# w_o by paired quarters, norm steps at fixed points, w_down by thirds of columns, and activations in eight DRAM buffers

## The chip, the cores and the metric

The kernel runs on one core of a Trainium2 chip. The metric is the device time of one execution in microseconds (us); less is better. The time before is the median of three executions. One further execution was recorded by the hardware profiler, and the trace and all rows shown are from that one.

## What is computed

One step of a one-layer decoder block on 1024 prompt rows and 8 x 4 sample rows, 1056 rows of 1024 values in all, in float32. The part that the change touches begins at `w_o`:

```python
def _rmsnorm(x, g):
    xf = x.astype(jnp.float32)
    y = xf * lax.rsqrt(jnp.mean(xf * xf, axis=-1, keepdims=True) + EPS)
    return (y * g.astype(jnp.float32)).astype(x.dtype)
...
    x = x + (g_a * y_a + g_b * y_b + g_m * y_m) @ w_o
    h = _rmsnorm(x, norm_ffn_g) @ w_up
    hc, conv_f_state = _causal_dwconv3(h, conv_f_prev, conv_f_w)
    hc = hc + conv_f_b
    a, gt = jnp.split(hc, 2, axis=-1)
    x = x + (jax.nn.silu(gt) * a) @ w_down
...
y_prompt = _rmsnorm(xp, norm_final_g)
```

`w_o` is 1024 x 1024, `w_up` 1024 x 5632, `w_down` 2816 x 1024. Ahead of this stand the input projections, a short convolution, a gated spatial mix and attention over 256 memory rows; the change leaves them as they are.

## The kernel before

**Matrix products.** Activations lie transposed: `S`, `zhi` and `zlo` hold 128 partitions x 8 feature tiles x 1056 rows. A float32 product is done as three float32r products. A weight tile is loaded to `ws`, ScalarE casts it to `wh` (L188), VectorE subtracts to get the rest `wl` (L190), and `three` (L210) issues `wh*xhi`, `wh*xlo` and `wl*xhi` (L211 to L213). So each weight unit costs one DMA on SyncE's queue, one ScalarE cast and one VectorE subtraction. `unit_cols` lists the units in order of use, `load_unit` loads them into a ring of three, `split_unit` casts them, `split_lows` subtracts, and `ahead` runs two units before use.

**What sets the order.** The program is written out by hand, and each engine and each DMA queue works through its own list in that order. Small items are put into a queue `aux` and taken out by `weave` between groups of matmuls, at a rate that `pace` sets; in the FFN, items are taken at fixed products.

**w_o.** Eight output tiles f of 128 columns. f 0 to 3 come first, each over three chunks of 352 rows (`main(wo_evac(f))`). `wo_evac` adds x (brought back from DRAM by `x_back`, L1067, on ScalarE's DMA queue), squares the sum on ScalarE and adds it to `acc` on GpSimd. f 4 to 7, whose split weights were kept in `wo`, follow by quarters of 264 rows in the order 0, 2, 1, 3, two tiles to one PSUM pair (`wo_pair`).

**The norm (`norm2`).** When a quarter is done, its items enter `aux`: `total` (L1216: TensorE sums the squares over partitions), `spread` (L1228: TensorE lays 1/rms over all partitions), `scale` (L1246, VectorE), and `parts` (L1254 cast on ScalarE, L1255 subtraction on VectorE). The FFN's product with `w_up` uses a scheme of seven products of half-size blocks in place of eight, so the quarters 2 and 3 also make differences of blocks (`minus`, L1259, GpSimd). `spread`'s PSUM tile and the outputs of `parts` are read by products 1 to 7 later on.

**The FFN.** There are 24 entries of seven products in the order `ORDER`; entries 0 to 3 are half entries (columns 0 and 1, for the first row half, then the second), the other 20 cover both. For each entry `raw_load` brings four blocks of `w_up`, `sums` makes three combinations on GpSimd (L1337 to L1339), `prepare` casts and subtracts four products ahead (L1350, L1351) and makes one more difference on GpSimd (L1354). `evacuate` moves products out of PSUM (L1444, L1446), `conv_items` is the convolution (L1386 to L1407), `gate_items` is the gate (L1419, L1420, L1424) and the store of an activation row to DRAM (`act_d`, L1425).

**w_down.** Four quarters of 264 rows; for each, four pairs of output tiles (q) by six groups of up to four activation rows (g), so 4 x 24 = 96 weight units. `stage_items` loads a group from `act_d` (L1530), and x from `x_d` with the fifth group (L1534); `part` casts and subtracts it (L1543, L1544). For the first quarter the groups are staged in two rows of `S` while the FFN's last entry runs (`at_last`).

**The end (`finish`).** Per quarter three pieces of 88 rows: eight transposes (L1615), a square with sum (L1619), `scales` (L1633, then `rsqrt`, L235 to L241), and the output multiply (L1644) and store. The last quarter's pieces run after the last product.

## Time and profile before

| | us |
|---|---|
| median of three executions | 1943.39 (1943.14 to 1945.38) |
| the profiled execution | 1948.35 |
| its span, first to last instruction | 1946.6 |
| TensorE busy in it | 1853.6 (95%) |
| VectorE | 1199.1 (62%) |
| ScalarE | 662.7 (34%) |
| GpSimd | 391.4 (20%) |

The span is cut into 40 equal slices below; each digit is the busy share of a slice in tenths (9 is 90% or more), and PEclk is the TensorE clock that was granted.

```profile
PE   8999999999999999999999667999999996999997
DVE  5576775328533753366361668898888886556654
PEclk9999999999999999999999887999999998999998
```

A slice is 48.7 us. TensorE (PE) is busy throughout except in the 23rd to 25th slice (1071 to 1217 us), where w_o ends, the norms run and the FFN begins, in the 34th (1606 to 1655), between the FFN and w_down, and at the two ends. The 23rd and the 24th slice, and the 25th, also have a lower clock.

### The profile page before, as it was taken

The numbers are of one execution on the slowest core, as the hardware profiler recorded it, in microseconds if no ns is written. First come the engines' busy times: TensorE is split into PE (matmuls) and PEld (weight loads), VectorE is DVE, ScalarE is ACT, GpSimd is POOL, SyncE is SP. The second block draws the span as 40 slices with busy tenths as digits, with TensorE's granted clock in tenths as the row PEclk, the third lists the DMA queues.
The fourth block names the chain that finished last, engine by engine and source line by source line (L and its number), as shares of the span: only waits on it lengthen the run. The fifth ranks groups of instructions, "written<-read, shape, count | busy, mean of one in ns | idle before, by whom it ended". The sixth has DMA issues, their size and how long they took to land.

```text
span 1946.6 us, 32112 instructions
## 1 busy us (share of the span) xinstructions
PE 1853.6 (95%) x13032; PEld 1824.7 (94%) x13032; DVE 1199.1 (62%) x2200; ACT 662.7 (34%) x1078; POOL 391.4 (20%) x475
## 2 busy tenths in 40 slices
PE   8999999999999999999999667999999996999997
PEld 8988999999999999999999667999999996899997
DVE  5576775328533753366361668898888886556654
ACT  6644313221322132112341223333433433344443
POOL 2221200000000000000002435665656651000000
PEclk9999999999999999999999887999999998999998
DMA  8736152133212521252141112322322315776764
GB/s 260 202 111 228 52 178 76 44 108 121 76 47 66 173 74 40 61 166 77 57 134 61 45 60 77 88 74 72 90 73 73 90 56 169 255 238 201 244 193 124
DMA packets 263443, 225.59 MB, mean 116 GB/s; under 512 B 8272, under 2 KB 248472, under 8 KB 263296
## 3 DMA queue, kind: packets, MB, share of 16 engines
q1 hardware_dynamic: 253383, 209.97, 35.4%
q10 hardware_dynamic: 9913, 13.57, 2.1%
q8 instruction: 102, 1.67, 0.4%
q14 instruction: 45, 0.37, 0.1%
HBM read 193.71 MB, written 29.81 MB: 115 GB/s over the span
## 4 chain that ended last, share of the span: by engine, by line
PE 60%; DVE 11%; POOL 10%; issue 9%; DMA 5%; ACT 4%; SPq 1%; ACTq 0%; DVEq 0%; POOLq 0%
PE mm L213 14%; PE mm L211 14%; PE mm L212 14%; PE pair L213 3%; PE pair L211 3%; PE pair L212 3%; DMA ws<-in_w_down 3%; POOL rs L1420 2%; POOL S L1339 2%; DVE wh L1351 2%; DVE wl L190 2%; POOL S L1338 1%; POOL S L1337 1%; POOL ext L1390 1%; POOL ws L1354 1%
## 5 line engine op out<-in xcount | busy, mean ns | idle before, releaser
L211 PE MATMUL mm<-zhi,wh 128*128 128x352 f32 x1824 | 591.9, 324 | 0.3 <-ACT zhi L273 0.3
L212 PE MATMUL mm<-zlo,wh 128*128 128x352 f32 x1824 | 589.5, 323 | 1.1 <-POOL zlo L284 1.0
L213 PE MATMUL mm<-zhi,wl 128*128 128x352 f32 x1824 | 588.4, 323 | 0.2 <-DVE wl L190 0.2
L190 DVE TENSOR_TENSOR wl<-ws,wh 128x1024 fp32r<-128x1024 f32 (+1 forms) x203 | 245.0, 1209 | 217.3 <-ACT wh L188 216.3
L211 PE MATMUL pair<-zhi,wh 128*128 128x264 f32 x1152 | 332.9, 289 | 24.0 <-ACT wh L188 17.0
L212 PEld LDWEIGHTS mm<-zlo,wh 128*128 128x128 f32 x1824 | 342.5, 188 | 2.7 <-POOL zlo L284 1.9
L211 PEld LDWEIGHTS mm<-zhi,wh 128*128 128x128 f32 x1824 | 343.1, 188 | 1.2 <-ACT zhi L273 0.6
L213 PEld LDWEIGHTS mm<-zhi,wl 128*128 128x128 f32 x1824 | 342.7, 188 | 0.5 <-DVE wl L190 0.5
L212 PE MATMUL pair<-zlo,wh 128*128 128x264 f32 x1152 | 331.2, 287 | 0.4 <-DVE zlo L1544 0.4
L188 ACT CAST wh<-ws 128x1024 fp32r<-128x1024 f32 x204 | 206.2, 1014 | 275.1 <-PE mm L212 101.8
L211 PEld LDWEIGHTS pair<-zhi,wh 128*128 128x128 f32 x1152 | 220.7, 192 | 25.4 <-ACT wh L188 17.4
L212 PEld LDWEIGHTS pair<-zlo,wh 128*128 128x128 f32 x1152 | 220.6, 192 | 0.6 <-DVE zlo L1544 0.6
L213 PE MATMUL pair<-zhi,wh 128*128 128x264 f32 x704 | 202.6, 288 | 0.0
L211 PE MATMUL pair<-fs,wh 128*128 128x264 f32 x536 | 158.1, 295 | 10.8 <-DVE rs L1444 6.1
L213 PEld LDWEIGHTS pair<-zhi,wh 128*128 128x128 f32 x704 | 135.3, 192 | 0.0
L213 PE MATMUL pair<-zhi,wl 128*128 128x264 f32 x448 | 128.9, 288 | 3.0 <-DVE wl L190 2.9
L211 PEld LDWEIGHTS pair<-fs,wh 128*128 128x128 f32 x536 | 102.8, 192 | 14.5 <-ACT wh L188 4.1
L844 DVE CUSTOM_DVE_ANT_0 qr<-fs,fs 128x256 f32<-128x256 f32 x256 | 108.4, 423 | 7.3
L212 PE MATMUL pair<-fs,wh 128*128 128x264 f32 x384 | 110.0, 286 | 0.0
L212 PE MATMUL pair<-rs,wh 128*128 128x264 f32 x356 | 102.4, 288 | 0.0
L213 PE MATMUL pair<-fs,wh 128*128 128x264 f32 x352 | 100.3, 285 | 0.0
L1130 ACT ACTIVATE sig<-mm 128x352 f32<-128x352 f32 x72 | 33.4, 464 | 186.9 <-PE mm L213 186.6
(334 smaller groups left out, 3200.6 us busy)
## 6 DMA issues: line engine op xcount, KB each, us to landing
ws<-in_w_in SPq DMA_DIRECT2D x88, 512.0 KB
ws<-in_w_down SPq DMA_DIRECT2D x80, 512.0 KB
fs<-q_d SPq DMA_DIRECT2D x32, 512.0 KB
ws<-in_w_up SPq DMA_DIRECT2D x54, 256.0 KB
act_d<-rs SPq DMA_DIRECT2D x21, 528.0 KB
S<-in_w_up SPq DMA_DIRECT2D x42, 256.0 KB
fs<-in_cache_mem_k SPq DMA_DIRECT2D x16, 512.0 KB
fs<-in_cache_mem_v SPq DMA_DIRECT2D x16, 512.0 KB
```

What stands on the lines that cost most here:

```text
L188: nc.scalar.copy(out=hi, in_=t)
L190: lows.append(lambda: eng.tensor_tensor(out=lo, in0=t, in1=f32(hi), op=ALU.subtract))
L211: mmul(ps, lhsT=wh, rhs=xh, start=first, stop=False)
L212: mmul(ps, lhsT=wh, rhs=xl, start=False, stop=False)
L213: mmul(ps, lhsT=wl, rhs=xh, start=False, stop=last)
L844: nc.vector.tensor_tensor_reduce(out=att["qr"], in0=q[:, i, :], in1=t[:, 2 * (bb % 2) + mt, :], scale=1.0, scalar=0.0, op0=ALU.mult, op1=A ...
L1130: nc.scalar.activation(out=t, in_=ps, func=AF.Sigmoid)
L1337: tt(out=s1, in0=a21, in1=a22, op=ALU.add)
L1338: tt(out=s2, in0=s1, in1=a11, op=ALU.subtract)
L1339: tt(out=a21, in0=a11, in1=a21, op=ALU.subtract)
L1351: nc.vector.tensor_tensor(out=lo, in0=a, in1=f32(hi), op=ALU.subtract)
L1420: nc.gpsimd.tensor_tensor(out=g[:, :T], in0=g[:, :T], in1=outs[j, 0][:, :T], op=ALU.mult)
```

## The change

Five parts, all behind the input projections.

1. **w_o by paired quarters.** Instead of four tiles over three chunks, then four tiles over four quarters, there are 32 steps of one tile and one quarter (24 matmuls of 264 columns). First quarters 0 and 2: tiles 0 to 3 in pairs of quarters, then tiles 4 to 7 for quarter 0 and for quarter 2. Then the same for quarters 1 and 3, for which tiles 0 to 3 are loaded and split a second time.
2. **Norm steps at fixed points.** `total`, `spread` and the other items stand at numbered steps (a table `todo` for w_o's steps, `ffn_first` for the FFN's products) and no longer in `aux`. For quarters 1 and 3, two of the four block differences run on VectorE.
3. **The FFN's order and places.** Products 2 and 6 change places; raw weights, sums and sigmoids of entries 4 and later lie in whole rows of `S`; entry 3 is handled like the entries before it.
4. **w_down by thirds.** Three thirds of 352 rows instead of four quarters: 72 weight units, not 96, and matmuls of 352 columns. `act_d` is eight tiles of up to three activation rows each, x is laid out in another way and is read back later, and the staged groups are eight of three rows.
5. **The end.** Pieces of 128, 128 and 96 rows, 9 in all instead of 12. The last three pieces share one `scales`, and two halves of their outputs are made by ScalarE and GpSimd and stored from ScalarE's queue.

The core of the diff:

```diff
-    for f in range(4):
-        unit_cols(w_o, f * P)
+    for f in range(8):
+        unit_cols(w_o, f % 4 * P)
...
-            head = [total, no, spread, scale(0, 0), scale(0, 1)]
             if not second:
-                return head + [parts(1, b11), scale(1, 0), scale(1, 1), parts(2, b21)]
-            return head + [
-                minus(b11, b12, b11),
+                return total, spread, [
+                    scale(0, 0), scale(0, 1), scale(1, 0), scale(1, 1), parts(1, b11), parts(2, b21)
+                ]
+            dve = nc.vector if s else nc.gpsimd
+            return total, spread, [
+                scale(0, 0), scale(0, 1),
+                minus(b11, b12, b11, dve),
                 scale(1, 0), scale(1, 1),
                 parts(3, b22),
-                minus(b12, b22, b12),
+                minus(b12, b22, b12, nc.gpsimd),
+                minus(b22, b22, b11, dve),
+                parts(6, b22),
                 parts(5, b11),
-                minus(b22, b22, b11),
+                minus(b21, b21, b22, nc.gpsimd),
                 parts(7, b12),
-                minus(b21, b21, b22),
-                parts(6, b22),
                 parts(4, b21),
             ]
 
...
+        def wo_pairs(f, s, ps):
+
+            until(lambda: len(back) == 3)
+            x = halves(S[:, f, :], s)
+            a = halves(acc[:, :T], s)
+            nc.vector.tensor_tensor(out=x, in0=ps[:, :, :QC], in1=x, op=ALU.add)
+            if f == 0:
+                nc.scalar.activation(out=a, in_=x, func=AF.Square)
+            else:
+                sq = squares()
+                nc.scalar.activation(out=sq, in_=x, func=AF.Square)
+                nc.gpsimd.tensor_tensor(out=a, in0=a, in1=sq, op=ALU.add)
+
...
-        ORDER = (1, 6, 2, 5, 7, 3, 4)
+        ORDER = (1, 2, 6, 5, 7, 3, 4)
...
-                    t = t[:, :, 0:P], t[:, :, P : 2 * P]
+                if half and e >= 4:
+                    t = v3(S[:, 6 + e % 2, :], KT, P)
...
-        act_d = dram.tile([NJ, P, T], F32, name="act_d")
-        x_d = dram.tile([4, P, KT, QC], F32, name="x_d")
+        act_d = [dram.tile([3, P, T], F32, name=f"act_d{i}") for i in range(8)]
+        x_d = dram.tile([P, KT, T], F32, name="x_d")
...
-        for f in range(4):
-            main(wo_evac(f))
-        drain()
...
+        norms = {c: norm2(c) for c in range(4)}
+
+        def plan_norm(at, c, first=0):
+
+            total, spread, items = norms[c]
+            slots = {(at, 2): [total], (at + 1, 2): [spread]}
+            for i, x in enumerate(items):
+                slots[at + 2 + i // 3, i % 3] = [x]
+            return slots
+
+        todo = {}
+        for at, c in ((12, 0), (16, 2), (28, 1)):
+            for key, gos in plan_norm(at, c).items():
+                todo.setdefault(key, []).extend(gos)
+        todo.setdefault((24, 0), []).append(lambda: sums(0))
+        todo.setdefault((22, 2), []).append(lambda: raw_load(0))
+        for i in range(6):
+            todo.setdefault((25 + i // 2, i % 2), []).append(lambda i=i: prepare(i + 1))
+
+        def wo_step(at, w, ps, c):
+            wh, wl = w
             r = quarter(c)
-            for f in (4, 6):
-                if f == 4:
-                    nc.sync.dma_start(out=x_d[c, :, 0:4, :], in_=S[:, 0:4, r])
-                ps = pair()
-                for x in range(2):
-                    wh, wl = wo[f + x]
-                    for k in range(KT):
-                        three(ps[:, x, :QC], wh[:, k, :], wl[:, k, :], zhi[:, k, r], zlo[:, k, r], k == 0, k == KT - 1)
-                        if k % 3 == 2:
-                            weave()
-                wo_pair(f, r, ps)
+            for k in range(KT):
+                three(ps, wh[:, k, :], wl[:, k, :], zhi[:, k, r], zlo[:, k, r], k == 0, k == KT - 1)
+                if k in (2, 5):
+                    split_lows()
+                    for go in todo.get((at, k // 3), ()):
+                        go()
+                    if at < 8:
+                        weave()
+
...
+        pace(24)
+        at = 0
+        for s in range(2):
+            order = [(f, c) for f in range(4) for c in (s, s + 2)]
+            if s == 0:
+                order = [(0, 0), (1, 0), (0, 2), (1, 2)] + order[4:]
+            ws, pss = {}, {}
+            if s:
+                drain()
+            for f, c in order:
+                if f not in ws:
+                    ws[f], pss[f] = next_unit(), pair()
+                    ahead()
+                wo_step(at, ws[f], pss[f][:, c // 2, :QC], c)
+                if c == s + 2:
+                    wo_pairs(f, s, pss[f])
+                wo_rest(at)
+                at += 1
+            for c in (s, s + 2):
+                nc.sync.dma_start(out=x_d[:, 0:4, quarter(c)], in_=S[:, 0:4, quarter(c)])
+            for c in (s, s + 2):
+                for f in range(4, 8):
+                    if f % 2 == 0:
+                        ps = pair()
+                    wo_step(at, wo[f], ps[:, f % 2, :QC], c)
+                    if f % 2:
+                        wo_pair(f - 1, c, ps)
+                        nc.sync.dma_start(out=x_d[:, f - 1 : f + 1, quarter(c)], in_=S[:, f - 1 : f + 1, quarter(c)])
+                    wo_rest(at)
...
-                    z = as4(st[g]) if c else block(S, g % 2, 3)
+                    st[g] = S[:, 6 + g % 2, :] if c == 0 else fs.get()
                     nc.sync.dma_start(
-                        out=z[:, :nk, :], in_=act_d[k0 : k0 + nk, :, quarter(c)].rearrange("k p t -> p k t")
+                        out=view(st[g], g),
+                        in_=act_d[g][: min(3, NJ - 3 * g), :, c * CH : (c + 1) * CH].rearrange("j p t -> p j t"),
                     )
-                    if g == 4:
-                        nc.sync.dma_start(out=S[:, :, quarter(c)], in_=x_d[c])
...
             go = {
-                1: [loads[0]], 6: [load_unit], 2: [splits[0], loads[2], load_unit],
-                7: [splits[2], loads[4], loads[1], load_unit], 3: [splits[1], loads[3]],
-                4: [splits[3], split_unit, split_lows],
+                1: [load_unit, load_unit, loads[0]],
+                5: [lambda: extra_free(6), splits[0], loads[1]],
+                7: [lambda: rows_free(0), load_unit, loads[2]],
+                3: [splits[1], loads[3], splits[2], loads[4], split_unit],
+                4: [lambda: extra_free(7), splits[3], split_lows, loads[5]],
             }
...
+        ffn_first = {}
+        total, spread, items = norms[3]
+        ffn_first[1] = [total]
+        ffn_first[3] = [spread]
+        for i, x in enumerate(items):
+            ffn_first.setdefault(4 + i, []).append(x)
+        POPS = {1: 1, 2: 2, 6: 1, 5: 1, 7: 1, 3: 1, 4: 1}
...
+            def x_again(c=c):
+                nc.sync.dma_start(out=S[:, :, c * CH : (c + 1) * CH], in_=x_d[:, :, c * CH : (c + 1) * CH])
+
             if c == 0:
-                at_slot(0, 0, left[0], splits[4])
-                for x, go in enumerate(left[1:]):
-                    at_slot(x // 5, x % 5, go)
-                at_slot(1, 2, loads[5])
-                at_slot(1, 4, splits[5])
+                for x, go in enumerate(left):
+                    at_slot(0, max(0, x - 3), go)
+                at_slot(0, 0, splits[4], loads[6])
+                at_slot(0, 1, splits[5])
+                at_slot(0, 2, splits[6])
+                at_slot(0, 4, loads[7])
+                at_slot(1, 1, splits[7])
+                at_slot(1, 2, x_again)
...
+                la = (12, 13, 14, 15, 16, 17, 19, 20) if c == 0 else (3, 5, 7, 9, 11, 13, 19, 20)
+                sa = (13, 14, 15, 16, 17, 18, 21, 22) if c == 0 else (5, 7, 9, 11, 13, 15, 21, 22)
+                for go, x in zip(nloads + nsplits, la + sa):
+                    at_slot(*divmod(x, 6), go)
...
-            scales(i)()
-            out(i, (slice(0, 512), slice(512, D)))()
+        scales(0, 3)()
+        for i in range(3):
+            out(i, ((0, 512, True), (512, D, i == 2)))()
```

Three places where the order of the instructions changes, each as the rows of one engine's or queue's list (source line, operation, out<-in, shape, xcount).

**ScalarE where w_o begins.** L1067 are the six DMAs that bring x back, L188 the casts of w_o's tiles 0 to 3, L1282 and L1299 the squares of tile 0. Before:

```order
L1067 DMA S<-xT_d 128x4x352 x2
L1130 ACTIVATE sig<-mm 128x352
L1150 CAST zhi<-S 128x4x352 x2
L188 CAST wh<-ws 128x1024
L1067 DMA S<-xT_d 128x4x352 x2
L1282 ACTIVATE fs_9653<-S 128x352 x2
L1067 DMA S<-xT_d 128x4x352 x2
L349 COPY fs_9721<-aux 72x128
L351 DMA out_new_conv_a_prompt<-fs_9721 2x4x128
```

And now:

```order
L1067 DMA S<-xT_d 128x4x352 x2
L1130 ACTIVATE sig<-mm 128x352
L1150 CAST zhi<-S 128x4x352 x2
L188 CAST wh<-ws 128x1024 x2
L1067 DMA S<-xT_d 128x4x352 x4
L1299 ACTIVATE fs_9653<-S 128x2x264
L1302 ACTIVATE fs_9654<-S 128x528
L188 CAST wh<-ws 128x1024
```

Two casts, of the third and the fourth tile, stand next to each other ahead of four of the six DMAs, where one cast stood ahead of two and the squares of two chunks ahead of the last two.

**GpSimd through w_o's end and the norms.** The additions of squares are L1286 and L1296 before, L1303 and L1313 now; the block differences L1259 and now L1251; `sums` L1337 to L1339 and now L1354 to L1356; the further difference L1354 and now L1371. Before:

```order
L1286 TENSOR_TENSOR fs_9653<-fs_9653,fs_9654 128x352 x9
L1296 TENSOR_TENSOR fs_9653<-fs_9653,fs_9654 128x264 x4
L1337 TENSOR_TENSOR fs_10266<-ws 128x4x128
L1338 TENSOR_TENSOR fs_10266<-fs_10266,ws 128x4x128
L1339 TENSOR_TENSOR ws<-ws 128x512
L1259 TENSOR_TENSOR S<-S 128x4x264
L1296 TENSOR_TENSOR fs_9653<-fs_9653,fs_9654 128x264 x2
L1259 TENSOR_TENSOR S<-S 128x4x264 x3
L1296 TENSOR_TENSOR fs_9653<-fs_9653,fs_9654 128x264 x2
```

And now:

```order
L1303 TENSOR_TENSOR fs_9653<-fs_9653,fs_9654 128x2x264 x3
L1313 TENSOR_TENSOR fs_9653<-fs_9653,fs_9654 128x264 x4
L1251 TENSOR_TENSOR S<-S 128x4x264
L1303 TENSOR_TENSOR fs_9653<-fs_9653,fs_9654 128x2x264
L1251 TENSOR_TENSOR S<-S 128x4x264 x3
L1303 TENSOR_TENSOR fs_9653<-fs_9653,fs_9654 128x2x264 x2
L1354 TENSOR_TENSOR fs_10447<-ws 128x4x128
L1355 TENSOR_TENSOR fs_10447<-fs_10447,ws 128x4x128
L1356 TENSOR_TENSOR ws<-ws 128x512
L1371 TENSOR_TENSOR ws<-ws,fs_10447 128x512
L1313 TENSOR_TENSOR fs_9653<-fs_9653,fs_9654 128x264 x4
```

The block differences of quarter 2 stand between the additions for tiles 0 to 3 of quarters 1 and 3, and the first entry's `sums` with the difference stand ahead of the additions (L1313) of quarters 1 and 3 for the tiles 4 and 5.

**The passage to w_down: ScalarE.** L1543 and now L1605 are the casts of staged activation groups, L188 those of w_down units, L1386 and now L1403 the convolution, L1419 and now L1436 the sigmoid. Before:

```order
L1543 CAST zhi<-S 128x4x264
L1350 CAST wh<-S 128x512
L1543 CAST fs_10319<-S 128x1056
L1419 ACTIVATE S<-rs_15901 128x4x264
L349 COPY fs_16013<-aux 72x128
L351 DMA out_new_conv_ffn_prompt<-fs_16013 2x4x128
L351 DMA out_new_conv_ffn_sample<-fs_16013 16x4x128
L1543 CAST zhi<-S 128x4x264
L1543 CAST fs_10632<-S 128x1056
L188 CAST wh<-ws 128x1024
L1386 ACTIVATE fs_16084<-rs_15968,vec 128x1056
L188 CAST wh<-ws 128x1024 x2
```

And now:

```order
L1605 CAST fs_10241<-S 128x1056
L1436 ACTIVATE S<-rs_16016 128x1056
L349 COPY fs_16122<-aux 72x128
L351 DMA out_new_conv_ffn_prompt<-fs_16122 2x4x128
L351 DMA out_new_conv_ffn_sample<-fs_16122 16x4x128
L1605 CAST rs_10794<-S 128x1056
L1605 CAST zhi<-S 128x1056
L188 CAST wh<-ws 128x1024
L1605 CAST zhi<-S 128x1056
L1403 ACTIVATE fs_16197<-fs_16047,vec 128x1056
L188 CAST wh<-ws 128x1024 x2
L1403 ACTIVATE fs_16279<-rs_16151,vec 128x1056
```

The first w_down cast stood behind four activation casts and now stands behind three.

**And SyncE's queue there.** L1530 and now L1594 load activation groups, L1534 loads x, L166 loads w_down units, L1425 and now L1442 store activation rows. Before:

```order
L1530 DMA S<-act_d 128x4x264
L166 DMA ws<-in_w_down 128x4x256
L1530 DMA S<-act_d 128x4x264
L166 DMA ws<-in_w_down 128x4x256
L1530 DMA S<-act_d 128x4x264
L1534 DMA S<-x_d 128x8x264
L1530 DMA S<-act_d 128x4x264
L166 DMA ws<-in_w_down 128x4x256
L1530 DMA S<-act_d 128x4x264
```

And now:

```order
L166 DMA ws<-in_w_down 128x4x256 x2
L1594 DMA S<-act_d_9655 128x3x352
L1594 DMA S<-act_d_9656 128x3x352
L166 DMA ws<-in_w_down 128x4x256
L1594 DMA S<-act_d_9657 128x3x352
L1594 DMA S<-act_d_9658 128x3x352
L1594 DMA S<-act_d_9659 128x3x352
L1442 DMA act_d_9661<-rs_16016 128x1056
L1594 DMA S<-act_d_9660 128x3x352
```

The load of x (L1534) is no longer among these; two w_down units are loaded ahead of the first activation group, and each load reads from a buffer of its own.

More of the change, by code (lines that the diff above doesn't have):

```diff
@@ L1586, in layer_step @@
                     late.popleft()()
-            for _ in range(2 if e < 2 else 1):
-                if aux and (e < 2 or n in (1, 7)):
-                    aux.popleft()()
+            if e > 3 and aux and n in (1, 7):
+                aux.popleft()()
             product(e, n)
+            for go in ffn_first.pop(at, ()):
+                go()
             if 1 in ss:
@@ L1656, in layer_step @@
         late.clear()
-        for c in range(4):
+        for c in range(3):
             turn, scales, out = finish(c)
```

237 lines of the change are left out of this document (115 added, 122 removed).

## The prediction, made before the change was run

> **What bounds the kernel now.** I read the span first, then a table of the seven stretches that the change touches (columns: stretch, us; busy time and instruction count of TensorE's matmuls, its weight loads, VectorE, ScalarE, GpSimd; granted clock; DMA share; GB/s).
>
> ```profile
> span 1946.6 us, 32112 instructions
> ```
> ```profile
> 1013.10:1059.50 46.40, 45.78 (x288) 45.40 (x286) 13.89 (x19) 10.72 (x18) 7.53 (x8) 1.00 0.36 117
> 1059.50:1146.60 87.10, 60.02 (x428) 59.28 (x429) 46.12 (x75) 20.23 (x28) 25.93 (x17) 0.83 0.17 56
> 1146.60:1216.20 69.60, 53.01 (x341) 51.50 (x341) 56.74 (x76) 24.84 (x39) 40.62 (x33) 0.79 0.22 62
> 1216.20:1631.20 415.00, 414.04 (x3372) 411.25 (x3372) 359.97 (x461) 156.53 (x230) 242.66 (x296) 1.00 0.27 79
> 1631.20:1647.20 16.00, 0.35 (x4) 0.14 (x2) 4.07 (x4) 3.19 (x4) 2.19 (x10) 0.65 0.71 237
> 1647.20:1933.40 286.20, 276.17 (x2205) 272.92 (x2205) 162.89 (x197) 126.53 (x154) 2.52 (x1) 0.98 0.70 216
> 1933.40:1946.60 13.20, 0.91 (x7) 0.49 (x5) 7.26 (x25) 1.80 (x9) 0.00 (x0) 0.61 0.26 82
> ```
>
> In order they are w_o's first four tiles, its last four with the norms, FFN entries 0–3, entries 4–23, the passage to w_down, w_down, and the tail. TensorE is the bound in the first, the fourth and nearly all of the sixth. In the second and third it is idle or slowed for much of the time, and in the fifth it does nothing. The profiled execution took 1948.35 us, 1.75 more than its span and 5.0 more than the median of 1943.39; I take the sum off the first and carry the difference to the median.
>
> Everything ahead of 1013 stays as it is.
>
> **w_o and its norms (133.5 us now).** What a matmul costs by its width:
>
> ```profile
> 1030.03 0.32 PE L212 MATMUL mm<-zlo,wh 128*128 128x352 f32 x1
> ...
> 1033.89 0.32 PE L212 MATMUL mm<-zlo,wh 128*128 128x352 f32 x1
> ```
> ```profile
> 1838.36 0.29 PE L212 MATMUL pair<-fs,wh 128*128 128x264 f32 x1
> ...
> 1842.48 0.28 PE L213 MATMUL pair<-fs,wl 128*128 128x264 f32 x1
> ```
>
> The first two rows are 24 starts apart: 3.86/24 = 0.161 us for 352 columns. The second two are 34 apart: 4.12/34 = 0.121 for 264. By column they are equal, so 288 x 0.161 + 384 x 0.121 = 92.9 us before and 768 x 0.121 = 92.9 after. The width gains nothing. Of 133.5 us the rest, 40.6, is waiting and slow matmuls. The largest wait, with one of its four places and the matmuls behind it:
>
> ```profile
> PE aux L1216 <- DVE fs L1296: 27.1, 4, 11.3
> ```
> ```profile
> 1120.86 1.01 PE L1216 MATMUL aux<-ones,fs 128*88 128x1 f32 x6 [11.27 <-DVE fs L1296]
> ...
> 1122.10 0.42 PE L212 MATMUL pair<-zlo,rs 128*128 128x264 f32 x1
> 1122.32 0.42 PE L213 MATMUL pair<-zhi,rs 128*128 128x264 f32 x1
> ```
>
> TensorE waits for the sum of squares of the quarter it has just finished, 27.1 us over four quarters, and the matmuls behind a long wait start 0.22 apart, not 0.121. The sum is late because VectorE and GpSimd are still in the norm of the quarter before:
>
> ```profile
> 1105.79 10.23 POOL L1259 TENSOR_TENSOR S<-S 128x1056 f32<-128x1056 f32 x3
> ```
> ```profile
> 1110.41 8.01 DVE L1255 TENSOR_TENSOR fs<-S,fs 128x1056 fp32r<-128x1056 f32 x3
> ```
>
> Side by side they take 3.41 and 2.67 us apiece. After the change each total stands 24 matmuls (2.9 us) behind its quarter, was 9 (1.1 us), and the norm of quarters 0 and 2 spreads over steps 12 to 22 of 32, with eight steps on the four tiles loaded again before the next quarter is due. I expect the totals of quarters 0 and 2 on time. The added price is four unit loads, ScalarE casts and lows; VectorE is 46.1 busy of 87.1, so they hide unless that cover is gone, and then cost some 1.2 us each.
>
> New waits. First, x's rows come back late. They are issued by ScalarE, and took 6.4 us:
>
> ```profile
> 1022.14 1.91 ACTq L1067 DMA_DIRECT2D S<-xT_d  x2
> ```
> ```profile
> 1028.59 0.53 DVE L1280 TENSOR_TENSOR S<-mm,S 128x352 f32<-128x352 f32 x1 [6.54 <-DMA S<-xT_d]
> ```
>
> Now four of the six issues stand behind the cast of the fourth weight tile, which waits for a buffer that step 2 frees, at 1013.1 + 3 x 2.9 = 1021.8. The cast ends near 1023, two issues and 6.4 us on the way later it is 1031.3, and the add of tile 0 is done at 1032. TensorE needs that accumulator at step 6, at 1030.5 or a little later: about 2 us of wait (with 1 lost to the clock, as behind the short waits quoted under w_down; between 0 and 6 in all). Second, quarter 1's total. GpSimd has three sums of the first FFN weights and a difference ahead of that quarter's additions:
>
> ```profile
> L1338 POOL TENSOR_TENSOR S<-S,ws 128x512 f32<-128x512 f32 x4 | 6.3, 1584 | 0.3
> ```
>
> The loads go out behind step 22 and land 6.4 us later, 3.5 into step 24. Three sums take 4.7, the wait for two lows on VectorE at least 2, the difference 1.6, four additions 3.0, VectorE's own two about 1.5: 16.3 us from the start of step 24, and the total stands behind step 28, at 5 x 2.9 = 14.5. That is 2 us late, and 7 where sums and lows run side by side at the longer times above; I take 5 (between 0 and the 11.3 seen). With 0.9 for the start, 3.3 for the totals and spreads themselves, 0.6 for tail transposes and 2 for slow matmuls the excess is 14.8, so 107.7 us: **-25.8**.
>
> **FFN entries 0–3 (69.6).** Their 336 matmuls need 336 x 0.121 = 40.7; VectorE is busy for 56.74 and is nearest to the bound. The norm of the last quarter stays here: its total moves behind the second product, its parts behind products 4 to 16. VectorE's work stays about the same; one of its items now waits for two GpSimd subtractions at 3.41 = 6.8 us, and I leave 3.6 for the start: 56.7 + 6.8 + 3.6 = 67 (between 50, TensorE's time with a third of its 28.9 us of idle left, and 74, where the 6.8 is added to today's): **-2.6**.
>
> **Entries 4–23 (415.0).** Same matmuls, same operations by count; only the homes of raw weights, sums and sigmoids move to whole rows, and products 2 and 6 change places. TensorE is busy for 414.0 of 415.0, so no gain beyond a few us is there. VectorE's time lies beside it, with room left by waits such as this one:
>
> ```profile
> L1424 DVE TENSOR_TENSOR rs<-rs,S 128x1056 f32<-128x1056 f32 x20 | 25.1, 1255 | 35.4 <-POOL rs L1420 35.4
> ```
>
> I take **-1** (411 to 418).
>
> **Passage to w_down (16.0).** ScalarE's last steps ahead of the first w_down matmul, and the queue that feeds them:
>
> ```profile
> 1639.10 1.07 ACT L1543 CAST zhi<-S 128x1056 fp32r<-128x1056 f32 x1 [9.36 <-DMA S<-act_d]
> 1645.08 1.07 ACT L1543 CAST fs<-S 128x1056 fp32r<-128x1056 f32 x1 [4.91 <-DMA S<-act_d]
> 1646.05 1.04 ACT L188 CAST wh<-ws 128x1024 fp32r<-128x1024 f32 x1
> ```
> ```profile
> 1630.33 0.60 SPq L1534 DMA_DIRECT2D S<-x_d  x1
> 1630.97 0.65 SPq L1530 DMA_DIRECT2D S<-act_d  x1
> ...
> 1641.49 0.36 SPq L1530 DMA_DIRECT2D S<-act_d  x1
> ```
>
> The first w_down cast stands behind the fourth activation cast, whose load went out behind the 1 MB load of x and landed 14 us later. After: eight buffers, so a load waits only for its own three rows; x is loaded in the second quarter of the first third; and the first w_down cast stands behind the third activation cast alone. Two staging rows still alternate, so the third load waits for the first split. I expect the first unit's data before entry 23 ends, and leave 3 us for the last evacuation, a cast (1.04) and a low (about 1.2): **-13** (between 0 and 16 left).
>
> **w_down (286.2).** 2112 x 0.121 = 255.6 before, 1584 x 0.161 = 255.0 after. Transposes:
>
> ```profile
> L1615 PE MATMUL pair<-ident,S 128*88 128x128 f32 x91 | 12.0, 272 | 0.0
> ```
>
> 91 become 66: 12.0 to 8.7. What is left, 286.2 - 255.6 - 12.0 = 18.6, is waiting for weights and slow matmuls:
>
> ```profile
> 1821.60 0.39 PE L211 MATMUL pair<-fs,wh 128*128 128x264 f32 x1 [1.82 <-ACT wh L188]
> ...
> 1823.90 0.42 PE L211 MATMUL pair<-fs,wh 128*128 128x264 f32 x1
> ```
>
> The first waits 1.82 us, and 2.3 us later matmuls take 0.42 instead of 0.28: a short wait costs clock as well. The Trainium skill, "TensorE: Matmul & The Clock Gate", section "What's actually happening", has the clock halve only after an idle window of about 3.4 us; by that, waits under 3 us would cost only themselves, and the sum would be 1 us lower in w_o and about 2 lower here, some 1885. This trace doesn't agree at this place (1.82 us of idle, then 0.42 us a matmul).
>
> Each 512 KB unit now feeds 24 matmuls of 3.86 us, not 2.9; 24 of 96 units go, with their loads, casts and lows, and the DMA share of 0.70 falls by about a quarter of its weight part. The waits don't go altogether: activation loads and splits, 16 staged groups behind the first third, still come in bunches. I take 11.3 of 18.6 (2 to 20): 275, **-11.2** (266 to 284).
>
> **Tail (13.2).**
>
> ```profile
> L1644 DVE SCALAR_TENSOR_TENSOR rs<-pair,st,rs 88x512 f32<-88x512 f32 x4 | 2.8, 742 | 0.2
> ```
> ```profile
> L235 ACT ACTIVATE st<-st 88x1 f32<-88x1 f32 x3 | 0.6, 203 | 4.8 <-DVE st L1633 4.8
> ```
>
> Three scale chains of some 1.35 us in turn become one (2.7 less), and two of six output multiplies (1.5 less) go to ScalarE and GpSimd; but the one chain now stands behind all three squares (2.0 more). **-2.2** (9.5 to 13.5).
>
> Sum: -25.8 - 2.6 - 1 - 13 - 11.2 - 2.2 = -55.8. On the profiled execution 1892.5; on the median 1887.6.
>
> **Rivals.**
> - *The totals go on waiting.* For: VectorE and GpSimd still slow each other in the norms. Against: the next quarter's steps now lie between. If three of the four wait as before, about 20 us come back: 1908. Chance 0.13.
> - *The first FFN entries become TensorE-bound.* For: 28.9 of their 69.6 us are idle on TensorE. Against: VectorE is busy for 57. 50 us there, 17 less: 1871. Chance 0.15.
> - *Short waits cost no clock.* For: the mean clock is 0.98 in w_down in spite of its waits. Against: the slow matmuls behind 1.82 us. The 1 us at x's return and 2 of the 11.3 in w_down go: 1885. Chance 0.05.
> - *The passage keeps its wait.* For: two staging rows, and splits in turn on ScalarE. Then 13 come back: 1901. Chance 0.08.
> - *Slower: the steady entries lengthen.* An entry takes 20.75 us and VectorE is busy 18.0 of it, 2.75 idle. Whole-row homes could make more VectorE operations run beside GpSimd at the price above (2.67 instead of 1.25, 1.4 more for one of 1056 columns). From two such per entry VectorE is the bound; the gain is gone at 55.8/20 = 2.8 us per entry beyond that, that is with four more per entry. At 5.8 more per entry less 2.75 idle it is 61 us: 1949. Nothing in the order adds such pairs. Chance 0.03.
> - *It doesn't do what it says* (the extra unit loads starve TensorE in w_o, all other gains lost): 1943, 0.02.
>
> **How the numbers follow.** The forecast has 0.54. Its own range is 1875 to 1900: half spans of about 6, 5, 3, 4, 8 and 1 us for the six terms, added as squares, make 12. The rivals on the same side lie at 1871, 1885, 1901 and 1908, each as wide, so 1868 to 1910 leaves out about half of the first, a third of the last, and the two on the other side: 0.17. A measurement of this kernel can tell about 0.2% (3.9 us) from no change. Faster by more: 0.95; within: 0.02; slower: 0.03.
>
> **What would show it.** Right: no wait over 3 us at the totals of quarters 0 and 2, one of about 5 at quarter 1's; TensorE's gap ahead of w_down near 3 us; w_down near 275 with fewer waits for casts; steady entries still at 20.75. Wrong: totals that wait 5 us or more each; an idle passage over 8 us; VectorE above 18.5 us per entry; w_down still above 282, which would mean that its waits are not set by the weight units' number.

## The result and the profile after

| | us |
|---|---|
| before, median (1943.14 to 1945.38, 4 runs) | 1943.74 |
| after, median (1889.29 to 1890.46, 4 runs) | 1890.01 |
| ratio, 95% interval | 0.972 (0.971 to 0.974) |
| predicted | 1887.6 (1868 to 1910) |
| profiled execution after; its span | 1889.29; 1887.5 |

The changed kernel cut into the same stretches as before (stretch, us; busy time of TensorE's matmuls, weight loads, VectorE, ScalarE, GpSimd; granted clock; DMA share; GB/s):

```profile
1012.30:1120.80 108.50, 100.76 (x807) 100.27 (x808) 57.85 (x88) 31.61 (x43) 31.74 (x22) 0.95 0.35 112
1120.80:1186.70 65.90, 48.46 (x351) 47.06 (x350) 51.65 (x82) 25.41 (x40) 31.90 (x31) 0.87 0.23 69
1186.70:1602.40 415.70, 414.29 (x3372) 411.88 (x3370) 359.40 (x461) 157.03 (x231) 244.13 (x298) 1.00 0.27 81
1602.40:1605.10 2.70, 0.03 (x1) 0.00 (x0) 2.12 (x2) 2.02 (x2) 0.02 (x1) 1.00 0.20 32
1605.10:1875.20 270.10, 265.06 (x1653) 264.25 (x1653) 135.49 (x154) 102.77 (x122) 4.56 (x11) 0.98 0.60 194
1875.20:1887.50 12.30, 0.89 (x7) 0.52 (x5) 4.55 (x13) 2.77 (x9) 2.52 (x2) 0.64 0.34 117
```

They are w_o with its norms, FFN entries 0 to 3, entries 4 to 23, the passage, w_down and the tail. w_o starts 0.8 us earlier than before (1012.3 against 1013.1; in the runs below it starts at 1012.2 to 1013.8). The kernel before was profiled a second time (the first experiment below); its column stands beside the first.

| stretch | before, first / second profile | after | change predicted | change measured, by first / second |
|---|---|---|---|---|
| w_o and norms | 133.5 / 131.3 | 108.5 | -25.8 | -25.0 / -22.8 |
| entries 0–3 | 69.6 / 69.5 | 65.9 | -2.6 | -3.7 / -3.6 |
| entries 4–23 | 415.0 / 415.0 | 415.7 | -1 | +0.7 / +0.7 |
| passage | 16.0 / 15.7 | 2.7 | -13 | -13.3 / -13.0 |
| w_down | 286.2 / 285.2 | 270.1 | -11.2 | -16.1 / -15.1 |
| tail | 13.2 / 13.1 | 12.3 | -2.2 | -0.9 / -0.8 |
| sum | 933.5 / 929.8 | 875.2 | -55.8 | -58.3 / -54.6 |

Between the medians the change is 53.7 us.

What TensorE waits for from 1000 us on in the changed kernel (us in all, times, longest):

```profile
PE pair L211 <- DVE rs L1461: 12.0, 4, 7.4
PE aux L1217 <- DVE fs L1313: 6.9, 1, 6.9
PE pair L213 <- DVE wl L190: 5.0, 1, 5.0
PE pair L211 <- DVE S L1461: 4.3, 2, 3.9
PE pair L211 <- ACT wh L188: 2.7, 1, 2.7
```

Before, the totals waited four times, 27.1 us; now once, 6.9 us, at quarter 1. The 4.3 and 10.6 of the 12.0 lie in FFN entries 0 to 3. From the passage to the end there was, before:

```profile
PE pair L211 <- ACT wh L188: 20.7, 4, 15.6
PE pair L213 <- DVE wl L190: 4.4, 7, 0.8
```

The 15.6 is the passage, and the first unit's low took 0.7 more. Now TensorE waits 2.7 us for the first unit's cast (L188) and, two matmuls into w_down, 5.0 for its low (the rest `wl`, which VectorE subtracts at L190). So the two waits for that unit went from 16.3 to 7.7 us, although the stretch called passage shows 2.7: it ends at the first matmul. The low is late because VectorE's list has the low of the fourth activation group ahead of it:

```profile
1608.28 1.26 DVE L1606 TENSOR_TENSOR zlo<-S,zhi 128x1056 fp32r<-128x1056 f32 x1 [1.08 <-ACT zhi L1605]
1609.45 1.22 DVE L190 TENSOR_TENSOR wl<-ws,wh 128x1024 fp32r<-128x1024 f32 x1
```

Behind the first 12 us of w_down no wait for weights is left.

### The profile page after: what moved, and what is told of

Its sections match the earlier page's. It is cut to its first block, busy times and chain, and to the rows that moved or that the text cites. A ratio compares the mean times of both kernels' runs of the same rounds, so it can differ in the third digit from the quotient of the medians.

```text
span 1887.5 us, 31072 instructions
## 1 busy us (share of the span) xinstructions
PE 1831.9 (97%) x12576; PEld 1807.1 (96%) x12576; DVE 1159.2 (61%) x2144; ACT 640.9 (34%) x1045; POOL 384.8 (20%) x475
## 5 line engine op out<-in xcount | busy, mean ns | idle before, releaser
L211 PE MATMUL mm<-zhi,wh 128*128 128x352 f32 x1728 | 560.9, 325 | 0.3 <-ACT zhi L273 0.3
L212 PE MATMUL mm<-zlo,wh 128*128 128x352 f32 x1728 | 558.1, 323 | 1.0 <-POOL zlo L284 1.0
L190 DVE TENSOR_TENSOR wl<-ws,wh 128x1024 fp32r<-128x1024 f32 x183 | 223.3, 1222 | 221.9 <-ACT wh L188 221.6
L211 PE MATMUL pair<-zhi,wh 128*128 128x264 f32 (+1 forms) x1096 | 326.0, 297 | 14.1 <-DVE rs L1461 8.8
L212 PE MATMUL pair<-zlo,wh 128*128 128x264 f32 (+1 forms) x1096 | 322.9, 295 | 0.0
L188 ACT CAST wh<-ws 128x1024 fp32r<-128x1024 f32 (+1 forms) x184 | 187.3, 1020 | 256.6 <-PE pair L212 97.5
L213 PE MATMUL pair<-zhi,wh 128*128 128x264 f32 x704 | 201.3, 286 | 0.0
L211 PE MATMUL pair<-fs,wh 128*128 128x264 f32 (+1 forms) x396 | 119.8, 303 | 3.1 <-ACT wh L188 2.7
L213 PE MATMUL pair<-zhi,wl 128*128 128x352 f32 (+1 forms) x392 | 121.4, 310 | 0.0
L212 PE MATMUL pair<-fs,wh 128*128 128x264 f32 (+1 forms) x396 | 118.5, 299 | 0.0
L211 PE MATMUL pair<-rs,wh 128*128 128x264 f32 (+1 forms) x352 | 104.7, 297 | 4.3 <-DVE rs L1461 3.2
L212 PE MATMUL pair<-rs,wh 128*128 128x264 f32 (+1 forms) x352 | 104.8, 298 | 0.0
```

The lines of the kernel that those rows point to most:

```text
L188: nc.scalar.copy(out=hi, in_=t)
L190: lows.append(lambda: eng.tensor_tensor(out=lo, in0=t, in1=f32(hi), op=ALU.subtract))
L211: mmul(ps, lhsT=wh, rhs=xh, start=first, stop=False)
L212: mmul(ps, lhsT=wh, rhs=xl, start=False, stop=False)
L213: mmul(ps, lhsT=wl, rhs=xh, start=False, stop=last)
```

## The experiments

Each run below is one execution with a profile, the last one five timed rounds. Executions of the changed kernel took 1889.3 to 1890.5 us; those of the kernel before, over all runs of this study, 1942.0 to 1948.9. So a single execution that lies a microsecond or two from 1890 says little by its time; what it shows is in its trace.

**1. The kernel before once more.** No edit.

> The unchanged kernel, profiled once more. Its first profiled execution took 1948.35 us, 5.0 above its median; that of the changed kernel took 1889.29, 0.7 under its median. Theory: the 5 us are one execution's late weights, so this trace is near 1943 us and the stretch of w_down takes about 281 us, not 286.2; the other stretches agree within 0.5 us. Rival: a profile of this kernel always costs 5 us, and the trace is near 1948 again; then the gain read from the traces (59.1 us) overstates the measured one (53.7) for good.

1944.65 us. Two stretches of both traces, behind the short wait at quarter 0's total. First profile:

```profile
1074.20:1079.00 4.80, 4.80 (x32) 4.80 (x32) 0.96 (x6) 0.33 (x2) 0.00 (x0) 0.71 0.30 103
```

Second profile:

```profile
1074.20:1079.00 4.80, 4.80 (x43) 4.80 (x44) 1.54 (x8) 0.27 (x2) 0.00 (x0) 1.00 0.30 103
```
```profile
PE aux L1216 <- DVE fs L1296: 27.1, 4, 11.3
```

The theory was mostly wrong: w_down is 1.0 us shorter, not 5. The largest part, 2.2 us, lies in w_o. The waits there are the same to a tenth (27.1), but behind the same short wait 43 matmuls ran in 4.8 us instead of 32, at a clock of 1.00 and not 0.71. So the first profile was of one of the longer executions within the usual spread, and its gains read 3.7 us too large; the right-hand figures of the table are the fairer ones.

**2. Quarter 1's additions on VectorE.**

```diff
-                eng = nc.gpsimd if f == 4 else nc.vector
+                eng = nc.gpsimd if f == 4 and c % 2 == 0 else nc.vector
```

> The additions of squares of tiles 4 and 5 run on VectorE for quarters 1 and 3 (as those of tiles 6 and 7 do), no longer on GpSimd. Theory: quarter 1's total waits 6.9 us because these additions stand on GpSimd behind the sums of the first FFN weights; the wait falls below 1.5 us, the 2.4 us of slow matmuls behind it go, and the execution takes about 1880 us. Rival: ScalarE's squares or VectorE's own queue are as late; the wait stays over 5 us and the execution over 1885.

1889.5 us, and the wait hardly moved:

```profile
PE aux L1217 <- DVE fs L1313: 6.5, 1, 6.5
```

So GpSimd's additions alone don't make that total late: in the changed kernel they end at 1105.0, and VectorE is not at its own last additions before 1107.0. VectorE's timeline of the changed kernel shows what it does until then (start, duration, instruction, idle before):

```profile
1100.53 2.73 DVE L1368 TENSOR_TENSOR wh<-fs,wh 128x512 fp32r<-128x512 f32 x2 [1.28 <-ACT wh L1367]
1103.18 2.37 DVE L1368 TENSOR_TENSOR wh<-ws,wh 128x512 fp32r<-128x512 f32 x2
1105.47 0.69 DVE L1308 TENSOR_TENSOR S<-pair,S 128x528 f32<-128x528 f32 x1
1107.01 0.90 DVE L1313 TENSOR_TENSOR fs<-fs,fs 128x264 f32<-128x264 f32 x2 [0.84 <-ACT fs L1310]
```

The last four of six lows of the first FFN weights (L1368) stand in VectorE's list ahead of the add of tiles 6 and 7 (L1308), at some 1.3 us each; TensorE is at the total from 1108.06 - 6.93 = 1101.1 on.

**3. Totals 9 matmuls behind, as before.**

```diff
-            slots = {(at, 2): [total], (at + 1, 2): [spread]}
+            slots = {(at, 0): [total], (at + 1, 2): [spread]}
```

> In w_o the totals of quarters 0, 2 and 1 stand 9 matmuls behind their quarter, as before the change, and not 24; all else is as changed. Theory: what made the old totals wait was VectorE and GpSimd busy with the quarter before, so now only the short chain behind the last matmul (add 0.7, square 0.64, two additions 0.43 each, with hand-overs about 2.5 us against 1.1 of cover) shows: waits of 1 to 2 us at quarters 0 and 2, 8 to 9 at quarter 1, 1892 to 1895 us. Rival: the distance itself was the gain; waits of 5 us or more at quarters 0 and 2, over 1900. Second rival: neither matters, 1890.

1897.72 us. The totals of quarters 0, 2 and 1:

```profile
1051.66 0.60 PE L1217 MATMUL aux<-ones,fs 128*88 128x1 f32 x6 [1.54 <-DVE fs L1313]
```
```profile
1066.29 0.60 PE L1217 MATMUL aux<-ones,fs 128*88 128x1 f32 x6 [1.53 <-DVE fs L1313]
```
```profile
1113.18 1.01 PE L1217 MATMUL aux<-ones,fs 128*88 128x1 f32 x6 [8.87 <-DVE fs L1313]
```

The waits are as the theory had them: 1.5, 1.5 and 8.9 us. Before, these three totals waited 1.5, 4.7 and 11.3 us, 17.5 in all; with the old distance it is 11.9, with the new one 6.9. So the distance of 24 matmuls covers 5.0 us, and the rest of the change, which spreads the quarters' norms, another 5.6. The fourth wait of before, 9.6 us for quarter 3's total, stood in front of the FFN; it went when that total moved in among the FFN's products, and this run leaves it there, so it says nothing about those 9.6. The time is 2.7 us above the range expected, by 15 slow matmuls behind the second wait of 1.5 us and 15 behind the `spread` in the FFN (0.1 us lost by each).

**4. Block differences on VectorE.** All four of quarter 3, not two. (In the changed kernel quarter 3 is the only one with differences on VectorE; quarter 1 makes none.)

```diff
-                minus(b12, b22, b12, nc.gpsimd),
+                minus(b12, b22, b12, dve),
...
-                minus(b21, b21, b22, nc.gpsimd),
+                minus(b21, b21, b22, dve),
```

> All four block differences of quarter 3 run on VectorE instead of two on GpSimd. Theory: TensorE's wait of 7.4 us in FFN entry 1 comes from VectorE waiting for a difference on GpSimd that stands behind the sums of entry 2, whose weights land late; the wait falls below 3 us, entries 0 to 3 take about 59 us instead of 65.9, the execution 1882. Rival: VectorE is the bound there; the two more operations (1.25 us each) cost as much as the wait saves, 1887 to 1891.

1886.33 us. In the changed kernel GpSimd's list reads:

```profile
1144.10 1.31 POOL L1354 TENSOR_TENSOR S<-ws 128x512 f32<-128x512 f32 x1 [12.08 <-DMA ws<-in_w_up]
1145.49 1.28 POOL L1355 TENSOR_TENSOR S<-S,ws 128x512 f32<-128x512 f32 x1
1146.73 1.26 POOL L1356 TENSOR_TENSOR ws<-ws 128x512 f32<-128x512 f32 x1
1147.95 2.40 POOL L1251 TENSOR_TENSOR S<-S 128x1056 f32<-128x1056 f32 x1
```

The difference (L1251) stands behind three sums that waited 12.08 us for weights. With all four on VectorE TensorE's wait of 7.4 us goes (the longest of that row is 2.1; the one of 3.9 us for another product stays, at 3.8), and the stretch takes:

```profile
1120.90:1185.00 64.10, 49.00 (x350) 46.63 (x349) 55.34 (x85) 26.36 (x41) 30.16 (x29) 0.90 0.24 71
```

64.1 us, against 65.9 in the changed kernel's own trace and 67.5 to 68.3 in the five runs that leave this stretch and what feeds it alone (6 to 9 and 11). The mechanism is as supposed, the gain 2 to 4 us and not 7. The expected 59 us and 1882 were missed: VectorE is now busy 55.3 of 64.1, so the rival is partly right.

**5. First FFN lows later.**

```diff
-            todo.setdefault((25 + i // 2, i % 2), []).append(lambda i=i: prepare(i + 1))
+            todo.setdefault((28 + i // 2, i % 2), []).append(lambda i=i: prepare(i + 1))
```

> The casts and lows of the first six FFN weight forms move from steps 25 to 27 of w_o to steps 28 to 30, behind quarter 1's last additions. Theory, after the run that moved the additions to VectorE without effect: VectorE's own list makes quarter 1's total late, since six lows of 1.1 to 1.8 us each stand ahead of the add of tiles 6 and 7; the wait of 6.9 us falls below 1.5, the 2.4 us of slow matmuls behind it go, w_o takes about 99 us instead of 108.4, and the execution is 1880 to 1883 (some of it lost again if the first FFN products then wait). Rival: GpSimd's sums hold both up whatever stands where; the wait stays over 4 us, over 1887.

1885.53 us. w_o, and entries 0 to 3:

```profile
1013.80:1114.20 100.40, 97.90 (x807) 97.42 (x808) 52.72 (x87) 31.37 (x43) 30.64 (x22) 1.00 0.36 116
1114.20:1184.20 70.00, 49.46 (x350) 47.75 (x349) 53.52 (x85) 26.16 (x41) 32.15 (x31) 0.83 0.25 72
```

And two of TensorE's waits there:

```profile
PE aux L1217 <- DVE fs L1313: 2.6, 2, 1.8
PE pair L211 <- ACT rs L1246: 9.0, 1, 9.0
```

The mechanism holds: w_o loses 8.1 us, the wait at quarter 1's total falls to 1.8 (0.8 is quarter 3's), and the clock stays at 1.00. The 1.8 that are left come from GpSimd: VectorE's last two additions now wait 2.91 us for GpSimd's, which stand behind the three sums. The time of 1880 to 1883 was missed, because half is given back: TensorE waits 9.0 us in FFN entry 1, behind the same difference on GpSimd as in run 4.

**6. First w_down split early.**

```diff
-                3: [splits[1], loads[3], splits[2], loads[4], split_unit],
+                3: [split_unit, split_lows, splits[1], loads[3], splits[2], loads[4]],
```

> The cast and the low of the first w_down unit stand ahead of the second activation group's, no longer behind the third cast and the fourth low. Theory: the second wait at the passage (5.0 us for the low, behind the low of the fourth group, which waits for its load) goes with most of the 2.3 us of slow matmuls, w_down takes 263 to 265 us instead of 269.8, 1882 to 1885 in all. Rival: the second group's split is then late instead, by its load; the waits at the passage (3.0 + 5.0) stay over 6 together, over 1887.

1890.54 us: the rival. TensorE starts w_down 0.1 us behind the FFN and then waits at the second unit:

```profile
PE pair L211 <- ACT wh L188: 4.3, 1, 4.3
```

The second unit's cast stands on ScalarE behind the fourth group's cast, which waits 4.22 us for its load:

```profile
1609.09 1.07 ACT L1605 CAST zhi<-S 128x1056 fp32r<-128x1056 f32 x1 [4.22 <-DMA S<-act_d]
```

From the last FFN matmul to the last of w_down it is 273.3 us (272.8 in the changed kernel).

**7. One activation buffer.**

```diff
-        act_d = [dram.tile([3, P, T], F32, name=f"act_d{i}") for i in range(8)]
+        act_all = dram.tile([NJ, P, T], F32, name="act_d")
+        act_d = [act_all[3 * i : min(NJ, 3 * i + 3)] for i in range(8)]
```

> Activations go to one DRAM buffer again, with the same rows read by each load. Theory of the prediction: the eight buffers let a load wait for its own three rows alone; with one the passage's gap grows from 3.0 to 8 us or more, over 1894. Rival: a load waited for its own rows before as well (the waits are set by the ranges read and written), and the gap went because x's load and the fourth cast left the place: no change, 1888 to 1891.

1891.09 us, and the waits at the passage are those of the changed kernel:

```profile
PE pair L213 <- DVE wl L190: 5.2, 1, 5.2
PE pair L211 <- ACT wh L188: 2.6, 1, 2.6
```

The rival again: the eight buffers as such are worth nothing here.

**8. A load of x at the passage.** Added: two loads of 528 KB ahead of the third group's. (Before the change x's load stood behind the third group's.)

```diff
+        def x_early():
+            t = fs.get()
+            nc.sync.dma_start(out=v3(t, 3, CH), in_=x_d[:, 0:3, 0:CH])
+            fs.put(t)
...
-                7: [lambda: rows_free(0), load_unit, loads[2]],
+                7: [lambda: rows_free(0), load_unit, x_early, x_early, loads[2]],
```

> Added work: two loads of 528 KB of x into spare tiles, between the second and the third activation group's, about where x was loaded before the change. Nothing reads them. Theory: x's load in the same queue is what made the fourth group land 14 us late before; the passage's waits grow by 5 us or more, 1894 or over. Rival: the groups wait for the FFN's last gates and for staging rows, not for bytes in the queue; the passage stays within 1 us, 1888 to 1891.

1893.03 us:

```profile
PE pair L213 <- DVE wl L190: 5.5, 1, 5.5
PE pair L211 <- ACT wh L188: 5.0, 1, 5.0
```

The two waits are 10.5 us instead of 7.7. Neither side is as expected, and the 2.8 us are not the queue's alone. The spare tiles that the added loads fill are wanted right behind them: ScalarE's copy of the convolution state waits for one of them, ahead of the second group's cast, and VectorE waits 5.31 us for the other.

```profile
1603.92 0.26 ACT L349 COPY fs<-aux 72x128 f32<-72x128 f32 x1 [3.29 <-DMA fs<-x_d]
```

So 2.8 us is the price of these loads with their tiles; what x's bytes in the queue cost by themselves isn't shown.

**9. 96 weight units.** Added: 24 units handled and not used.

```diff
-                        unit_cols(w_down, q * 256, k0=k0, nk=nk, cols=256)
+                        for _ in range(1 + (g % 3 == 1)):
+                            unit_cols(w_down, q * 256, k0=k0, nk=nk, cols=256)
...
+                if g % 3 == 1:
+                    next_unit()
+                    ahead()
```

> Added work: in w_down 24 of the 72 weight units are loaded, cast and subtracted a second time and not used, so 96 units are handled as before the change; the matmuls are the same. Theory: the waits for casts and lows inside w_down (none is left behind its first 12 us) went because each unit now has 3.86 us of matmuls and not 2.9; with 96 units 8 us or more come back, w_down takes 278 to 284 us instead of 269.8, and the execution is over 1897. Rival: the waits came from the activation groups and x's loads in their old places; w_down stays under 273, 1889 to 1893.

1896.35 us; w_down:

```profile
1606.10:1882.20 276.10, 267.37 (x1653) 264.73 (x1653) 163.83 (x178) 127.41 (x146) 3.72 (x11) 0.98 0.74 235
```

6.0 us come back of the 15 to 16 that w_down lost, under the 8 expected. VectorE's and ScalarE's busy times are those of before (163.8 and 127.4 us against 162.9 and 126.5), and the bytes no fewer (235 GB/s against 216), so the load of units is back in full; it explains some 40% of the gain. Another 3.3 are the transposes by the prediction's count (12.0 to 8.7). What is left is about 6 by the table, and about 10 if the 5.0 us for the first low are counted to the passage. These runs don't explain it; the order of the groups' and x's loads is the nearest cause, and was not tried by itself.

**10. No second load; the end on VectorE.**

```diff
-    for f in range(8):
-        unit_cols(w_o, f % 4 * P)
+    for f in range(4):
+        unit_cols(w_o, f * P)
...
-                    ws[f], pss[f] = next_unit(), pair()
-                    ahead()
+                    ws[f], pss[f] = (wo[f + 4] if s else next_unit()), pair()
+                    if not s:
+                        ahead()
...
-            out(i, ((0, 512, True), (512, D, i == 2)))()
+            out(i, ((0, 512, True), (512, D, True)))()
```

> Two edits in stretches far apart. Left out: the second load, cast and low of w_o's tiles 0 to 3; quarters 1 and 3 use tiles 4 to 7's weights there instead. And the end's six output halves are all made by VectorE and stored from SyncE's queue. Theory for w_o: the four units lie beside other work; w_o stays at 108.4 +- 1 us. Rival: they hold VectorE or ScalarE up; w_o gets 2 us or more shorter. Theory for the end: the two halves on ScalarE and GpSimd (0.69 + 1.26 each, one behind the other) are what ends last, so all six on VectorE (0.67 each) end no later; 12.6 us +- 0.4 from the last matmul's start. Rival: they save the 1.5 us of the prediction; 13.8 or more.

1889.84 us. This kernel leaves out what quarters 1 and 3 need (they are multiplied by other tiles' weights), so only its times are of use. w_o and the tail:

```profile
1013.30:1119.60 106.30, 99.29 (x806) 98.94 (x807) 52.46 (x84) 27.88 (x39) 31.73 (x22) 0.97 0.30 100
1875.90:1888.10 12.20, 1.31 (x9) 0.77 (x7) 5.89 (x16) 1.40 (x7) 0.00 (x0) 0.66 0.35 118
```

w_o is 2.2 us shorter than in the changed kernel's trace, but that trace is at the upper end: in the five runs that leave w_o alone (6 to 9 and 11) it takes 107.3 to 108.2, so the gain is 1 to 2 us, between theory and rival. What differs between those runs is clock: behind the same wait of 6.9 to 7.0 us at quarter 1's total 12 to 23 matmuls run slow, here 12. What this run alone lacks is TensorE's wait for x's return (0.7 to 1.0 us in w_o of the others, 1.2 in run 6): x is there 8.1 us after its first issue and not 8.9. So the second load costs about 1 us, if the missing wait is its doing, which no run shows by itself. The tail is 12.2 against 12.3: what ScalarE and GpSimd took over gained nothing.

**11. The third group in a spare tile.**

```diff
-                    st[g] = S[:, 6 + g % 2, :] if c == 0 else fs.get()
+                    st[g] = fs.get() if c or g == 2 else S[:, 6 + (g + (g > 2)) % 2, :]
...
-                    if c:
+                    if c or g == 2:
```

> The third activation group for w_down is loaded into a spare tile, so the two staging rows serve the others and each load waits for one split less. Theory, after the run with the early first split, where the wait of 5 us came back at the second unit: the passage is set by the loads that wait for staging rows, the fourth group's above all; the low's wait of 5.0 us falls below 2 and w_down to 265 or less, 1884 to 1887. Rival: the spare tile comes free late, or the groups wait for the last gates; no change, 1888 to 1891.

1891.04 us. Inconclusive: the fourth group's cast came 2.0 us earlier (1605.2, was 1607.17), but with one spare tile fewer VectorE took one of the FFN's last products out of PSUM late. The tile for it was still being stored:

```profile
1604.90 0.71 DVE L1461 TENSOR_TENSOR rs<-pair,S 128x528 f32<-128x528 f32 x1 [5.62 <-DMA out_new_conv_ffn_sample<-rs]
```

So that wait took the place of the other. Whether the passage shortens with a tile that is really free stays open.

**12. Runs 4, 5 and the end of run 10 together.**

> Three edits together: the first six FFN lows at w_o's steps 28 to 30, all four block differences of quarter 3 on VectorE, and the end's six output halves on VectorE. Theory: they act in different places. The first alone took w_o from 108.4 to 100.4 us but gave 3 to 4 back in FFN entries 0 to 3, where TensorE waited 9.0 us behind a block difference on GpSimd; the second takes that wait away (entries 0 to 3 at 63 to 65 us, not 70); the third is worth 0.5. Together 1879 to 1882 us. Rival: entries 0 to 3 are set by the late loads of the second and third entries' weights, which the earlier start does not move; they stay at 69 or more, 1885 to 1887.

1881.85 us (1880.63 to 1883.28, 5 rounds); ratio to the kernel before 0.967 (0.966 to 0.969). w_o, entries 0 to 3:

```profile
1012.70:1114.80 102.10, 99.40 (x806) 98.91 (x807) 53.56 (x88) 31.35 (x43) 30.62 (x22) 0.98 0.36 116
1114.80:1179.40 64.60, 51.49 (x350) 49.10 (x349) 55.23 (x85) 25.85 (x41) 29.48 (x29) 0.87 0.26 76
```

The time and entries 0 to 3 are as expected. w_o is not at 100.4 again: the wait at quarter 1's total is the same 1.8 us, but 16 slow matmuls follow it here (1.6 us) and none did in run 5. Together the two stretches take 166.7 us, not 174.4. This kernel beats both others, the changed one by about 8 us (1890.01 to 1881.85).

## Why the prediction was right, and where not

The time was 2.4 us over the forecast, inside its range. The sum was closer than its terms, and that is partly luck: too much at the passage and in the tail was made up for by too little in w_down. The range was also narrower than its own terms allow: it counts entries 0 to 3 with a half span of 5 us and the passage with 4, where their stated bounds of 50 to 74 and 0 to 16 make 12 and 8.

- *The carry to the median.* "I take the sum off the first and carry the difference to the median" took 5 us for a property of profiling. The second profile shows that it was spread. By the medians the change is 53.7 us, by the two profiles 59.1 and 55.4, and the forecast was 55.8.
- *w_o, -25.8.* Size right (-25.0, or -22.8 against the second profile). Quarters 0 and 2 are on time, quarter 1 waits 6.9 us, predicted 5, with 2.4 of slow matmuls, predicted 2. The working behind the 5 had the wrong chain: it had GpSimd's sums ahead of the additions. Run 2 took those additions off GpSimd and the wait stayed at 6.5; run 5 moved VectorE's lows and it fell to 1.8. GpSimd's chain is there, but second: the 1.8 us that are left wait for it. x's return costs 0.8 us and no clock, predicted 3. That the matmul's width gains nothing holds.
- *Entries 0 to 3, -2.6.* 65.9 us against 67, and 67.5 to 68.3 in the five runs named above. VectorE did wait for a difference on GpSimd, 6.1 us against 6.8, but because GpSimd itself stood 12.1 us for weights, which the prediction had not seen.
- *Entries 4 to 23, -1.* +0.7; VectorE busy 359.4 as before, so the rival of longer entries never came near.
- *The passage, -13.* Right by the stretch (2.7 us left, predicted 3), but not by its own account. The 3 us were to hold the first unit's cast and its low; the cast is there after 2.7 us, and the low costs another 5.0, which fall into w_down. With both, 16.3 us became 7.7, so the gain is near 9. The step that failed: only ScalarE's list was followed, where the first cast stands behind the third group's; on VectorE the first low stands behind the fourth group's. And one reason was wrong: "so a load waits only for its own three rows" was given to the eight buffers, and run 7 shows that one buffer does the same. Of the gain, x's load can account for 2.8 us at the most as far as run 8 goes. That the rest is the order, the first cast behind three group casts and not four, was argued and not taken apart.
- *w_down, -11.2.* The mechanism is partly shown, and this is the term most mis-sized: the prediction kept 11.3 us of waits and slow matmuls, and 270.1 - 255.0 - 8.7 = 6.4 are there, all at the start. They are the wait of 5.0 for the first low and the slow matmuls behind it; further on no wait is left. By run 9 the number of units brings back 6.0.
- *Tail, -2.2.* -0.9. One scale chain did replace three, but the 1.5 us for two halves on ScalarE and GpSimd was an error: these run one behind the other, and the last store leaves from there.

```profile
1879.77 0.69 ACT L1719 ACTIVATE fs<-pair,y 128x512 f32<-128x512 f32 x1 [1.76 <-DVE fs L1715]
1881.89 0.37 ACTq L1722 DMA_DIRECT2D out_y_prompt<-fs  x1
1882.36 0.69 ACT L1719 ACTIVATE fs<-pair,y 128x512 f32<-128x512 f32 x1 [1.90 <-POOL fs L1720]
1884.41 0.36 ACTq L1722 DMA_DIRECT2D out_y_prompt<-fs  x1
```

ScalarE's second half waits behind its own store, which waits for GpSimd; the store at 1884.41 is the last, where VectorE alone, at 0.66 us from one to the next from 1878.9 on, would have been done with all six by about 1883. That alone wouldn't shorten the tail: in run 10, where VectorE makes all six, the stores go out one after another from SyncE's queue, the last of them 9.4 us into the tail against 9.2 here, and it takes 12.2 us.

Of three rivals a piece came true: of "The totals go on waiting" (one of the four waits), of "Short waits cost no clock" (x's return, 0.8 us of wait, cost none) and of "The passage keeps its wait" (7.7 of 16.3 us are still there). The start of the FFN did not become TensorE-bound: VectorE is busy for 51.7 of its 65.9 us and waits for weights and differences in the rest.

## What to carry to other kernels

Where an engine waits for a short chain, look at what else stands in the list of each engine of that chain, and not at the engine named alone: the total waited for VectorE, and the work ahead of it there (lows for a later stage) could be moved by three steps for 8 us, half of which came back as the next wait in line (run 5) until that was moved too (run 12). Where one stretch ends at a first matmul, look at the wait of the second as well. Added work needs tiles of its own, or it holds up whoever wants them next (runs 8 and 11). And profile the kernel before twice before its trace is taken as the base of a sum.

## What the hardware showed that was not expected

The clock behind the same wait differs from run to run. Behind 1.5 us of idle at quarter 0's total, the first profile of the kernel before had a clock of 0.71 over the next 4.8 us, the second 1.00, and of the two waits of 1.5 us in run 3 only the second one has slow matmuls behind it:

```profile
1067.92 0.28 PE L211 MATMUL pair<-zhi,wh 128*128 128x264 f32 x1
1068.05 0.28 PE L212 MATMUL pair<-zlo,wh 128*128 128x264 f32 x1
1068.17 0.35 PE L213 MATMUL pair<-zhi,wl 128*128 128x264 f32 x1
1068.32 0.42 PE L211 MATMUL pair<-zhi,wh 128*128 128x264 f32 x1
```

They set in 1.6 us after work has resumed (1066.75 to 1068.32). Over all traces of this study TensorE waits 18 times for 1.4 to 1.8 us at a `total` or a `spread`, and in 9 of these 12 to 16 slow matmuls follow, 1.2 to 1.6 us lost; in the other 9 none does. The Trainium skill, "TensorE: Matmul & The Clock Gate", section "What's actually happening", speaks of a free-running window of activity; with that, the same idle time can fall into one window or across two, and the traces agree in that the outcome changes from run to run (0.71 and 1.00). Where it has the clock halve only after some 3.4 us of idle, these rows differ: about 1.5 us were enough in 9 of 18 cases.
